# Hybrid decoder layer: the delta rule's queries and later keys projected with tokens in partitions

## The chip, the cores and the metric

The kernel runs on one core of one Trainium2 chip. Its time is device microseconds of one execution; the kernel before took 744.98 us (median of three runs, 744.90 to 745.07). One more execution was profiled, and all durations below come from it. The engines are TensorE (PE in the profile, its weight loads PEld), VectorE (DVE), ScalarE (ACT), GpSimd (POOL) and SyncE (SP); each works through its own instructions in order and they wait for each other by semaphores. SP, ACT and POOL also issue DMAs, each in the order of its own queue.

## The reference, cut to what matters

One decoder layer on 256 tokens of width 2048. The input is normed and multiplied by one wide matrix `w_in`; its columns feed a gated delta rule (8 heads of 128), a block-sparse attention (8 heads of 128) and two sigmoid gates. For the change only the delta rule's queries, keys and values matter:

```
h = rms_norm(x, pre_norm_w)                       # (256, 2048)
gdn_qkv, gdn_z, gdn_b, gdn_a, moba_qkv, moba_z, gate_a, gate_b = split(h @ w_in)
qkv = silu(causal_depthwise_conv(gdn_qkv, conv_w))   # 4 taps along the tokens, per channel
qa, ka, va = split(qkv)                           # 8 heads of 128 each
qa, ka = l2_normalize(qa), l2_normalize(ka)
oa = gated_delta_rule(qa, ka, va, beta, g)        # scores k.k and q.k, a triangular inverse, a recurrence
...
x + rms_norm((sigmoid(gate_a) * u_a + sigmoid(gate_b) * u_b) @ w_out, post_norm_w)
```

The convolution runs along the tokens with one weight per channel and tap, so the kernel wants channels in partitions and tokens along the free axis for it.

## The kernel before, in words

Every product is done in float32r with each operand split into a high and a low part, and three products are summed: high by high, high by low and low by high. The normed input stands in SBUF as `hT`: features in partitions, 16 blocks of 128 features (`KT`), and for each block 512 columns, 256 tokens of the high part and 256 of the low part. The weights come from DRAM in loads of up to 1 MB by SP (`raw`), three buffers in turn. `split` (L260) makes a high part by a copy on ACT (L265) and a low part by a subtraction on DVE (L266), each into one of three buffers, in pieces of 1024 elements a partition. Such a piece is called a split below; a projection of 512 columns of `w_in` has eight, two blocks of 128 features in each. ACT can fill a buffer again when PE has done the split that stood in it three splits ago.

There are two ways to project. `proj_t` (L397) takes 256 columns of `w_in`; the weights are stationary and `hT` streams past, so channels come out in partitions. For each of two heads and each feature block it issues one matmul of 512 columns (high weights by both parts of `hT`) and one of 256 columns (low weights by the high part). `proj_n` (L419) takes 512 columns of `w_in`; here the tokens of `hT` are stationary and the weights stream, so tokens come out in partitions, and for each feature block and each half of the tokens it issues three matmuls of 512 columns. Both accumulate in PSUM.

The delta rule's first four keys are projected at the start together with the norm (`a_k`, not touched). Its eight queries and last four keys go through `proj_t`, two heads at a time. `halves` (L540) adds the two halves of such an accumulator (a copy on ACT, L542, and an addition on DVE, L543); `conv_silu` (L547) multiplies by the norm's factor on DVE (L550), makes four taps (one on ACT, L553, three on DVE, L555) and a SiLU on ACT (L559). The values go through `proj_n` instead: `values` scales the two accumulators into `ga_[:, 2]` (ACT, L865), `by_feature` (L868) transposes them in blocks of 32 by 32 on DVE (L873), writes them to DRAM (`v_t_d`, POOL, L825) and reads them back with channels in partitions (POOL, L829), and `conv_silu` copies each head from there (ACT, L552). When a pair of queries is ready, `score_pair` (L589) splits keys and queries (`kq`, L593 and L594), transposes the queries for their norms, multiplies (`s`, three matmuls of 512 and three of 256 columns a head), scales the products into `gdn` (DVE, L656 to L674), and writes blocks of them to DRAM by four DMAs (`l_d`, POOL, L612), from which `inverse` later builds the triangular inverse on DVE.

The order of the work is the order in which the program is written, and it holds on every engine. The list `ORDER` (L58) gives the projections. Inside a projection `tick()` is called after each piece of it, eight times for 256 columns and sixteen for 512, and each queue of side work (`gq` for scores and inverse, `cq` for values and attention features, and others) is then asked whether its next step is due; a step says by `yield` how long to wait, where 1 is two calls. The waits are constants at the top of the file (`R_WAIT`, `C_WAIT1` to `C_WAIT3`, `SC_WAIT` and others) and are not touched.

Of the kernel before, what the change touches and what calls it, by code (L numbers as in the profile page):

```python
# [8 lines left out]
F32 = mybir.dt.float32  # L9
F32R = mybir.dt.float32r  # L10
BF16 = mybir.dt.bfloat16
AF = mybir.ActivationFunctionType
# [3 lines left out]
P = 128  # L16
# [27 lines left out]
C_WAIT2 = 2.5  # L44
C_WAIT3 = 1
# [10 lines left out]


ORDER = (  # L58
    "q0 mv0 zg0 q1 kq2 kq3 zg1 v0 zm0 v1 zm1 mk0 mk1 mv1 ga0 ga1 ga2 ua0 ua1"
).split()  # L60


# [43 lines left out]
def hybrid_layer(  # L106
# [15 lines left out]
    nc = tc.nc  # L122
    B, S, D = x.shape
    NT = S // P
    KT = D // P
# [29 lines left out]
    def acc_tile(name):  # L155
        return acc.tile([P, 512], F32, tag="acc", name=name)
# [11 lines left out]
    def tick():  # L168
        after[0] -= 0.5
        for q in (gq, vq, mq, aq, bq, *extra):  # L170
            q.tick()
# [3 lines left out]
    def mm(*args, **kwargs):  # L175
        return pin(nc.tensor.matmul(*args, **kwargs))  # L176
# [83 lines left out]
    def split(raw, shape, name):  # L260
        splits[0] += 1
        pool = fourth[0] if fourth and splits[0] % 4 == 0 else wspl
        hi = pool.tile(shape, F32R, tag="hi", name=f"hi_{name}")
        lo = pool.tile(shape, F32R, tag="lo", name=f"lo_{name}")
        nc.scalar.copy(hi, raw)  # L265
        nc.vector.tensor_tensor(lo, raw, hi.bitcast(F32), op=ALU.subtract)  # L266
        return hi, lo
# [126 lines left out]
    na, dtb = nad[:, :H], nad[:, H:]  # L394


    def proj_t(col, name):  # L397

        pts = [acc_tile(f"a_{name}_{m}") for m in range(2)]
        for kb in range(2):  # L400
            raw = wraw.tile([P, 8, 256], F32, tag="raw", name=f"raw_{name}_{kb}")
            nc.sync.dma_start(
                raw, w_in[kb * 1024 : (kb + 1) * 1024, col : col + 256].rearrange("(k p) c -> p k c", p=P)
            )
            for m in range(2):
                hi, lo = split(raw[:, :, m * P : (m + 1) * P], [P, 8, P], f"{name}_{kb}_{m}")
                for k0 in range(0, 8, 2):
                    ks = range(k0, k0 + 2)
                    for kk in ks:
                        k = kb * 8 + kk  # L410
                        mm(pts[m], hi[:, kk, :], hT[:, k, :], start=(k == 0), stop=False)
                    for kk in ks:
                        k = kb * 8 + kk
                        mm(pts[m][:, :S], lo[:, kk, :], hT[:, k, :S], start=False, stop=(k == KT - 1))
                    if k0 % 4 == 2:
                        tick()
        return pts

    def proj_n(w, col, stat, nk, name, width=512, bank=acc_tile):  # L419

        pts = [bank(f"a_{name}_{t}")[:, :width] for t in range(NT)]
        for kb in range(nk // 4):
            raw = wraw.tile([P, 4, width], F32, tag="raw", name=f"raw_{name}_{kb}")
            nc.sync.dma_start(raw, w[kb * 512 : (kb + 1) * 512, col : col + width].rearrange("(k p) c -> p k c", p=P))
            for u in range(2):
                hi, lo = split(raw[:, 2 * u : 2 * u + 2, :], [P, 2, width], f"{name}_{kb}_{u}")
                for kk in range(2):
                    k = kb * 4 + u * 2 + kk
                    for t in range(NT):
                        sh = stat[:, k, t * P : (t + 1) * P]  # L430
                        sl = stat[:, k, S + t * P : S + (t + 1) * P]
                        mm(pts[t], sh, hi[:, kk, :], start=(k == 0), stop=False)
                        mm(pts[t], sh, lo[:, kk, :], start=False, stop=False)
                        mm(pts[t], sl, hi[:, kk, :], start=False, stop=(k == nk - 1))
                    tick()
        return pts
# [103 lines left out]
    def halves(pt, name):  # L540
        y = wf.tile([P, S], F32, tag="f256", name=f"y_{name}")
        nc.scalar.copy(y, pt[:, S:])  # L542
        nc.vector.tensor_tensor(y, pt[:, :S], y, op=ALU.add)  # L543
        return y

    def conv_silu(y, m, late=None, turned=None):
        xp = xps[xpi[0] % 3]  # L547
        xpi[0] += 1
        if turned is None:
            nc.vector.tensor_tensor(xp[:, NTAP - 1 :], y, rrow, op=ALU.mult)  # L550
        else:
            pin(nc.scalar.copy(xp[:, NTAP - 1 :].rearrange("p (t i c) -> p t i c", t=NT, i=4), turned))  # L552
        nc.scalar.activation(y, xp[:, 0:S], AF.Copy, scale=pcol[:, m : m + 1])  # L553
        for j in range(1, NTAP):
            nc.vector.scalar_tensor_tensor(  # L555
                y, xp[:, j : j + S], pcol[:, j * NCV + m : j * NCV + m + 1], y, op0=ALU.mult, op1=ALU.add
            )
        if late is None:
            nc.scalar.activation(y, y, AF.Silu)  # L559
        else:  # L560
            late.append(lambda: pin(nc.scalar.activation(y, y, AF.Silu)))
# [26 lines left out]
    def score_pair(h, kT, qT):  # L588
        kqs = []  # L589
        for m in range(2):  # L590
            kq = big.tile([P, 2, 2 * S], F32R, tag=("tt", "tw")[m], name=f"kq_{h + m}")
            for i, y in enumerate((kT[m], qT[m])):
                nc.scalar.copy(kq[:, i, :S], y)  # L593
                nc.vector.tensor_tensor(kq[:, i, S:], y, kq[:, i, :S].bitcast(F32), op=ALU.subtract)  # L594
            kqs.append(kq)
        yield Q_WAIT[h > 0]
        blocks = ga_[:, D // 512 - 1, h // 2 % 2]
        to = blocks.rearrange("p (j m t c) -> p m t j c", j=4, m=2, t=NT)
        for m in range(2):
            pin(nc.vector.transpose(to[:, m], qT[m].rearrange("p (t r j) -> p t j r", t=NT, j=4)))  # L600
        d = dram.tile([4, P, P], F32, name=f"q_d_{h}")
        nc.gpsimd.dma_start(d.rearrange("i (r j) x -> (i r) (j x)", j=4), blocks)
        q_ds.append(d)
        yield SC_WAIT - Q_WAIT[h > 0]

        for m in range(2):
            yield from scores(h + m, kqs[m])

        for b in range(4):
            t, p_ = b // 2, b % 2  # L610
            c0 = t * 4 * P + p_ * 64
            nc.gpsimd.dma_start(  # L612
                l_d[b, h : h + 2].rearrange("h j i -> j h i"),
                gsl[h // HG][p_ * 64 : p_ * 64 + 64, h % HG : h % HG + 2, c0 : c0 + 64],
            )
# [108 lines left out]

    kTs = [[] for _ in range(H // 2)]

    def keys(p):
        pk = proj_t(CK + 2 * p * P, f"k{2 * p}")
        kTs[p] += [halves(pk[m], f"k{2 * p + m}") for m in range(2)]
        for m in range(2):  # L730
            conv_silu(kTs[p][m], H + 2 * p + m)

    def queries(p):
        h = 2 * p
        pq = proj_t(CQ + h * P, f"q{h}")
        qTs = [halves(pq[m], f"q{h + m}") for m in range(2)]
        for m in range(2):
            conv_silu(qTs[m], h + m)
        gq.add(score_pair(h, kTs[p], qTs))
        if p == H // 2 - 1:  # L740
            gq.add(inverse())
            gq.add(solve())

# [110 lines left out]
            )  # L854

    v_left = [H // 2]

    cq = Queue()
    extra.append(cq)

    def values(g):
        pts = proj_n(w_in, CV + g * 512, hT, KT, f"v{g}")
        x = ga_[:, 2]
        for t in range(NT):
            nc.scalar.activation(x[:, t], pts[t], AF.Copy, scale=rstd[:, t : t + 1])  # L865
        cq.add(v_feat(g, x))

    def by_feature(name, x, blocks):  # L868
        yield C_WAIT1
# [11 lines left out]
    def v_feat(g, x):  # L881
        back = yield from by_feature(f"v{g}", x, ga_[:, 1])
        yield C_WAIT2
        for p in range(2):
            h = 4 * g + 2 * p
            after[0] = SLOW
            vTs = [wf.tile([P, S], F32, tag="f256", name=f"y_v{h + m}") for m in range(2)]
            for m in range(2):
                conv_silu(vTs[m], 2 * H + h + m, turned=back[:, 2 * p + m])
                yield C_WAIT3  # L890
            vq.add(v_tok(h, vTs))
            v_left[0] -= 1
# [529 lines left out]
    nq.add(query_norms())  # L1422
    for blk in ORDER:
        n, c = blk[:2].rstrip("0123456789"), int(blk[-1])
        if n in ("q", "kq"):
            if n == "kq":
                keys(c)
            queries(c)
        elif n in ("zg", "zm"):
            silu_gate(n, c)  # L1430
        elif n == "v":
            values(c)
        elif n == "mv":
            attention_values(c)
        elif n == "mk":
            attention(c)
        elif n == "ua":
            branch_pair(c)
        else:
            sigmoid_gate(n, {"ga": CGA, "gb": CGB}[n], c)  # L1440
# [285 lines left out]
```

## Time and profile before

| | |
|---|---|
| median of three runs | 744.98 us |
| profiled execution | 745.39 us |
| span of its profile | 743.7 us |
| PE busy | 734.3 us (99%), 3594 matmuls |
| DVE busy | 606.8 us (82%) |
| ACT busy | 456.1 us (61%) |
| POOL busy | 90.2 us (12%) |
| TensorE clock | 0.998 of full speed |

The span is what the profile covers, 1.7 us less than the execution's own time. A busy share of PE says that some matmul was under way, not that it ran at its peak: matmuls overlap, so the time that one takes from the next is the distance between their starts, and not the duration that its row gives. The distance is read from a stretch of the chain: its length divided by its matmuls.

### The profile page before, as it was taken

How to read it: one execution, taken by the hardware profiler on the slowest of the kernel's cores; microseconds unless marked ns; L12 is line 12 of the kernel's file. 1: busy time of each engine (PE TensorE's matmuls, PEld its weight loads, DVE VectorE, ACT ScalarE, POOL GpSimd, SP SyncE). 2: the span in 40 equal slices, each digit the busy share in tenths (PEclk: the TensorE clock that was granted, in tenths of full speed). 3: DMA queues.
4: the chain of work that ended last, by engine and by line, in shares of the span. 5: the costliest groups of instructions: out<-in, count | busy, mean ns of one | idle time of the engine just before them, and what ended most of it. 6: DMA issues, size and time to landing. Idle time of an engine off the chain costs nothing.

```text
span 743.7 us, 9927 instructions
## 1 busy us (share of the span) xinstructions
PE 734.3 (99%) x3594; PEld 620.7 (83%) x3594; DVE 606.8 (82%) x957; ACT 456.1 (61%) x692; POOL 90.2 (12%) x124
## 2 busy tenths in 40 slices
PE   9999999999999999999999999999999999999995
PEld 7898998899888888888888888888888888888885
DVE  6887779997896998988547889688797799898864
ACT  6777665556775665547556765657556653875751
POOL 1000301113100101232011050001000101110000
PEclk9999999999999999999999999999999999999999
DMA  8676586548867767988468789798988889998962
GB/s 290 206 233 223 167 239 199 171 153 249 289 215 238 251 200 266 309 295 289 158 216 313 260 301 281 223 343 231 344 224 314 231 299 284 378 346 224 276 244 113
DMA packets 94199, 187.49 MB, mean 252 GB/s; under 512 B 4421, under 2 KB 25606, under 8 KB 93638
## 3 DMA queue, kind: packets, MB, share of 16 engines
q1 hardware_dynamic: 76806, 134.83, 54.5%
q0 software_dynamic: 15584, 47.20, 21.8%
q10 hardware_dynamic: 1760, 4.83, 1.7%
q8 instruction: 28, 0.46, 0.2%
q14 instruction: 21, 0.17, 0.1%
HBM read 173.20 MB, written 13.64 MB: 251 GB/s over the span
## 4 chain that ended last, share of the span: by engine, by line
PE 98%; DMA 1%; DVE 0%; SPq 0%; ACT 0%; DVEq 0%; issue 0%
PE a_ga L176 12%; PE a_gb L176 12%; PE a_y L176 9%; PE a_ub L176 7%; PE a_zg L176 6%; PE a_k L176 6%; PE a_q L176 6%; PE a_mq L176 6%; PE a_mv L176 6%; PE a_mk L176 6%; PE a_v L176 6%; PE a_zm L176 6%; PE a_ua L176 5%; PE s L176 1%; PE po L176 1%; PE so L176 1%
## 5 line engine op out<-in xcount | busy, mean ns | idle before, releaser
L176 PE MATMUL a_ga<-hi_ga,hT 128*128 128x512 f32 x256 | 81.5, 393 | 0.0
L176 PE MATMUL a_gb<-hi_gb,hT 128*128 128x512 f32 x256 | 80.4, 389 | 0.0
L176 PEld LDWEIGHTS a_ga<-hi_ga,hT 128*128 128x128 f32 x256 | 48.1, 188 | 9.9
L176 PEld LDWEIGHTS a_gb<-hi_gb,hT 128*128 128x128 f32 x256 | 48.0, 188 | 9.9
L265 ACT CAST hi_gb<-raw_gb 128x1024 fp32r<-128x1024 f32 x32 | 33.6, 1054 | 29.3 <-PE a_gb L176 15.0
L266 DVE TENSOR_TENSOR lo_ga<-raw_ga,hi_ga 128x1024 fp32r<-128x1024 f32 x32 | 38.9, 1219 | 14.2 <-ACT hi_ga L265 13.9
L176 PE MATMUL a_ga<-lo_ga,hT 128*128 128x512 f32 x128 | 50.0, 390 | 0.0
L176 PE MATMUL a_gb<-lo_gb,hT 128*128 128x512 f32 x128 | 49.9, 390 | 0.0
L176 PE MATMUL a_zg<-hi_zg,hT 128*128 128x348 f32 (+1 forms) x192 | 46.7, 322 | 0.0
L265 ACT CAST hi_ga<-raw_ga 128x1024 fp32r<-128x1024 f32 x32 | 33.4, 1051 | 20.3 <-PE a_ga L176 16.7
L266 DVE TENSOR_TENSOR lo_gb<-raw_gb,hi_gb 128x1024 fp32r<-128x1024 f32 x32 | 38.7, 1215 | 6.9 <-ACT hi_gb L265 6.2
L176 PE MATMUL a_mv<-hi_mv,hT 128*128 128x512 f32 x128 | 41.6, 395 | 0.0
L176 PE MATMUL a_mk<-hi_mk,hT 128*128 128x512 f32 x128 | 40.5, 393 | 0.0
L176 PE MATMUL a_q<-hT,hi_q 128*128 128x512 f32 x128 | 40.2, 396 | 0.0
L176 PE MATMUL a_mq<-hi_mq,hT 128*128 128x512 f32 x128 | 39.8, 390 | 0.0
L176 PE MATMUL a_v<-hi_v,hT 128*128 128x512 f32 x128 | 39.8, 389 | 0.0
L176 PE MATMUL a_zm<-hi_zm,hT 128*128 128x512 f32 x128 | 39.8, 389 | 0.0
L176 PE MATMUL a_k<-hT,hi_k 128*128 128x512 f32 (+1 forms) x129 | 38.5, 398 | 0.7 <-ACT hi_k L297 0.6
L176 PEld LDWEIGHTS a_zg<-hi_zg,hT 128*128 128x128 f32 x192 | 33.5, 188 | 0.1
L266 DVE TENSOR_TENSOR lo_mv<-raw_mv,hi_mv 128x1024 fp32r<-128x1024 f32 x16 | 19.4, 1217 | 17.2 <-ACT hi_mv L265 16.0
L176 PE MATMUL a_zg<-lo_zg,hT 128*128 128x348 f32 (+1 forms) x96 | 30.9, 322 | 0.0
L265 ACT CAST hi_zg<-raw_zg 128x696 fp32r<-128x696 f32 (+1 forms) x24 | 18.5, 771 | 19.7 <-PE a_zg L176 7.4
(479 smaller groups left out, 2022.0 us busy)
## 6 DMA issues: line engine op xcount, KB each, us to landing
raw_ga<-in_w_in_dram SPq DMA_DIRECT2D x16, 1024.0 KB, 6.5
raw_gb<-in_w_in_dram SPq DMA_DIRECT2D x16, 1024.0 KB, 7.3
raw_y<-in_w_out_dram SPq DMA_DIRECT2D x14, 1024.0 KB, 8.7
raw_q<-in_w_in_dram SPq DMA_DIRECT2D x8, 1024.0 KB, 5.6
raw_mv<-in_w_in_dram SPq DMA_DIRECT2D x8, 1024.0 KB, 5.1
raw_v<-in_w_in_dram SPq DMA_DIRECT2D x8, 1024.0 KB, 5.1
raw_zm<-in_w_in_dram SPq DMA_DIRECT2D x8, 1024.0 KB, 5.2
raw_mq<-in_w_in_dram SPq DMA_DIRECT2D x8, 1024.0 KB, 6.2
```

Of the source, the lines that this page charges most:

```text
L176: return pin(nc.tensor.matmul(*args, **kwargs))
L265: nc.scalar.copy(hi, raw)
L266: nc.vector.tensor_tensor(lo, raw, hi.bitcast(F32), op=ALU.subtract)
```

## The change

`proj_t`, `keys`, `queries` and `values` go. One function `project(n, g)` takes their place: it projects four heads (512 columns of `w_in`) by `proj_n`, scales the two accumulators into `ga_` (ACT) and queues a generator. For values that is `v_feat` as before; for queries and keys it is the new `qk_feat`, which lets `by_feature` turn the four heads by DVE and DRAM, waits until the decays are done, and then runs `conv_silu` head by head from the block read back, with a step of waiting after each. A pair of queries then goes to `score_pair` as before. The keys have a queue of their own (`keyq`). `ORDER` puts queries 0 to 3, keys 4 to 7 and queries 4 to 7 first, and the values 0 to 3 between the gate blocks `zg0` and `zg1`.

```
 ORDER = (
-    "q0 mv0 zg0 q1 kq2 kq3 zg1 v0 zm0 v1 zm1 mk0 mk1 mv1 ga0 ga1 ga2 ua0 ua1"
+    "q0 k1 q1 mv0 zg0 v0 zg1 zm0 v1 zm1 mk0 mk1 mv1 ga0 ga1 ga2 ua0 ua1"
 ).split()
...
-    def proj_t(col, name):
-
-        pts = [acc_tile(f"a_{name}_{m}") for m in range(2)]
...
-    def keys(p):
-        pk = proj_t(CK + 2 * p * P, f"k{2 * p}")
-        kTs[p] += [halves(pk[m], f"k{2 * p + m}") for m in range(2)]
-        for m in range(2):
-            conv_silu(kTs[p][m], H + 2 * p + m)
-
-    def queries(p):
-        h = 2 * p
-        pq = proj_t(CQ + h * P, f"q{h}")
-        qTs = [halves(pq[m], f"q{h + m}") for m in range(2)]
-        for m in range(2):
-            conv_silu(qTs[m], h + m)
-        gq.add(score_pair(h, kTs[p], qTs))
-        if p == H // 2 - 1:
+    cq, keyq = Queue(), Queue()
+    extra += cq, keyq
+
+    def project(n, g):
+
+        pts = proj_n(w_in, {"q": CQ, "k": CK, "v": CV}[n] + g * 512, hT, KT, f"{n}{g}")
+        x = ga_[:, 0 if n == "k" else 2]
+        for t in range(NT):
+            nc.scalar.activation(x[:, t], pts[t], AF.Copy, scale=rstd[:, t : t + 1])
+        (keyq if n == "k" else cq).add(v_feat(g, x) if n == "v" else qk_feat(n, g, x))
+
+    def qk_feat(n, g, x):
+        back = yield from by_feature(f"{n}{g}", x, ga_[:, 1])
+        yield C_WAIT2
+        while decaying:
+            yield 0.5
+        for p in range(2 * g, 2 * g + 2):
+            h = 2 * p
+            ys = [wf.tile([P, S], F32, tag="f256", name=f"y_{n}{h + m}") for m in range(2)]
+            for m in range(2):
+                conv_silu(ys[m], (H if n == "k" else 0) + h + m, turned=back[:, h % 4 + m])
+                yield C_WAIT3
+            if n == "k":
+                kTs[p] += ys
+            else:
+                gq.add(score_pair(h, kTs[p], ys))
+        if (n, g) == ("q", 1):
             gq.add(inverse())
             gq.add(solve())
...
-    def values(g):
-        pts = proj_n(w_in, CV + g * 512, hT, KT, f"v{g}")
-        x = ga_[:, 2]
-        for t in range(NT):
-            nc.scalar.activation(x[:, t], pts[t], AF.Copy, scale=rstd[:, t : t + 1])
-        cq.add(v_feat(g, x))
...
-        if n in ("q", "kq"):
-            if n == "kq":
-                keys(c)
-            queries(c)
+        if n in ("q", "k", "v"):
+            project(n, c)
```

Three places of the instructions' order follow. The first is PE, at the start of the first query projection (`a_q_0` and `a_q_1` are its accumulators, `hT_166` the input, `hi_` and `lo_` the parts of the weights). Before:

```order
L176 MATMUL a_q_0_649<-hT_166,hi_q_0_0_653 128x512 x2
L176 MATMUL a_q_0_649<-hT_166,lo_q_0_0_654 128x256 x2
L176 MATMUL a_q_0_649<-hT_166,hi_q_0_0_653 128x512 x2
L176 MATMUL a_q_0_649<-hT_166,lo_q_0_0_654 128x256 x2
L176 MATMUL a_q_0_649<-hT_166,hi_q_0_0_653 128x512 x2
```

And now, at the same place:

```order
L176 MATMUL a_q_0_649<-hi_q_0_0_653,hT_166 128x512
L176 MATMUL a_q_0_649<-lo_q_0_0_654,hT_166 128x512
L176 MATMUL a_q_0_649<-hi_q_0_0_653,hT_166 128x512
L176 MATMUL a_q_1_650<-hi_q_0_0_653,hT_166 128x512
L176 MATMUL a_q_1_650<-lo_q_0_0_654,hT_166 128x512
L176 MATMUL a_q_1_650<-hi_q_0_0_653,hT_166 128x512
```

Two matmuls of 512 and two of 256 columns for two feature blocks of one head have become three of 512 columns for one feature block and half of the tokens, four heads wide.

The second place is POOL's queue around the first scores (`q_d` are queries for their norms, `l_d` blocks of the scores, `gdn` the scaled scores, `tv` an identity for the inverse). Before:

```order
L524 AFFINE_SELECT tv<-one 32x1024 x4
L602 DMA q_d_1102<-ga 128x512
L612 DMA l_d<-gdn_468 64x2x64 x4
L602 DMA q_d_1342<-ga 128x512
L612 DMA l_d<-gdn_468 64x2x64 x4
```

And now (`k_t_d` and `q_t_d` are the blocks of keys and queries that are turned by DRAM; the read-back into `ga` is the line after them or after `l_d`):

```order
L502 AFFINE_SELECT tv<-one 32x1024 x4
L816 DMA k_t_d<-ga 128x1024
L820 DMA ga<-k_t_d 128x4x256
L580 DMA q_d_1136<-ga 128x512
L816 DMA q_t_d<-ga 128x1024
L590 DMA l_d<-gdn_468 64x2x64 x4
L820 DMA ga<-q_t_d 128x4x256
L580 DMA q_d_1365<-ga 128x512
L590 DMA l_d<-gdn_468 64x2x64 x4
```

The write of queries 4 to 7 and their read-back stand on both sides of the first pair's four `l_d` writes; nothing of the kind was in this queue before the values.

The third place is ACT, where the queries behind the first scores are worked up (`hi_` are the casts of L265, `y_q` the queries in work, `kq` their split, `xp` the padded input of the taps). Before, from the last cast of one projection's weights on:

```order
L265 CAST hi_k_1_1_1328<-raw_k_1_1306 128x1024
L559 ACTIVATE y_q_1222<-y_q_1222 128x256
L593 CAST kq_1288<-y_q_1222 128x256
L559 ACTIVATE y_q_1225<-y_q_1225 128x256
L265 CAST hi_q_0_0_1374<-raw_q_0_1372 128x1024
```

And now, from the last cast of the block `mv0` to the first two of `zg0`:

```order
L265 CAST hi_mv_3_1_1399<-raw_mv_3_1373 128x1024
L530 COPY xp_159<-ga 128x256
L530 COPY xp_160<-ga 128x256
L531 ACTIVATE y_q_1391<-xp_159,pcol 128x256
L531 ACTIVATE y_q_1392<-xp_160,pcol 128x256
L265 CAST hi_zg_0_0_1443<-raw_zg_0_1441 128x696
L530 COPY xp_161<-ga 128x256
L531 ACTIVATE y_q_1467<-xp_161,pcol 128x256
L537 ACTIVATE y_q_1391<-y_q_1391 128x256
L537 ACTIVATE y_q_1392<-y_q_1392 128x256
L265 CAST hi_zg_0_1_1475<-raw_zg_0_1441 128x696
```

The copies from the read-back of queries 4 to 7 (`ga`) stand ahead of the first cast of `zg0`, where ACT had only work on data of PE and DVE before.

## Rows read from the trace of the kernel before

**Rows 1.** The page's chain that ended last, its shares by engine.

```profile
PE 98%; DMA 1%; DVE 0%; SPq 0%; ACT 0%; DVEq 0%; issue 0%
```

**Rows 2.** The chain in order of time: start us, length us, matmuls; five of PE's pieces.

```profile
48.58 11.16 PE a_q L176 x64
...
135.12 11.15 PE a_k L176 x64
...
159.51 7.64 PE a_zg L176 x48
...
198.69 21.76 PE a_zm L176 x96
...
263.97 22.02 PE a_mq L176 x96
```

**Rows 3.** The timeline of PE around one head's score products: start us, us, instruction.

```profile
104.28 1.21 PE L176 MATMUL s<-kq 128*128 128x512 f32 x6
105.32 0.63 PE L176 MATMUL a_q<-hT,hi_q 128*128 128x512 f32 x2
```

**Rows 4.** The timeline of ACT at the first values' read-back.

```profile
209.61 1.05 ACT L265 CAST hi_zm<-raw_zm 128x1024 fp32r<-128x1024 f32 x1 [1.66 <-PE a_zm L176]
211.18 0.41 ACT L552 COPY xp<-ga 128x256 f32<-128x256 f32 x1 [0.52 <-DMA ga<-v_t_d]
```

**Rows 5.** Groups of ACT's instructions: busy us, mean ns | idle us before.

```profile
L265 ACT CAST hi_mv<-raw_mv 128x1024 fp32r<-128x1024 f32 x16 | 16.8, 1051 | 13.1 <-PE a_mv L176 13.0
...
L553 ACT ACTIVATE y_q<-xp,pcol 128x256 f32<-128x256 f32 x8 | 4.1, 510 | 1.6 <-DVE xp L550 1.4
...
L593 ACT CAST kq<-y_q 128x256 fp32r<-128x256 f32 x8 | 3.3, 407 | 0.2
...
L552 ACT COPY xp<-ga 128x256 f32<-128x256 f32 x8 | 3.2, 399 | 0.5 <-DMA ga<-v_t_d 0.5
```

**Rows 6.** Groups of DVE's instructions, the same columns.

```profile
L266 DVE TENSOR_TENSOR lo_mv<-raw_mv,hi_mv 128x1024 fp32r<-128x1024 f32 x16 | 19.4, 1217 | 17.2 <-ACT hi_mv L265 16.0 <-PE a_mv L176 1.2
...
L266 DVE TENSOR_TENSOR lo_zg<-raw_zg,hi_zg 128x696 fp32r<-128x696 f32 x16 | 15.2, 956 | 4.5 <-ACT hi_zg L265 4.5
...
L555 DVE SCALAR_TENSOR_TENSOR y_q<-xp,pcol,y_q 128x256 f32<-128x256 f32 x24 | 11.1, 474 | 0.1
L873 DVE STREAM_TRANSPOSE ga<-ga 128x512 f32<-128x512 f32 x10 | 11.0, 1099 | 0.1
...
L666 DVE SCALAR_TENSOR_TENSOR gdn<-s,cj,dec 128x512 f32<-128x512 f32 x8 | 6.0, 749 | 0.2
...
L674 DVE SCALAR_TENSOR_TENSOR gdn<-s,cj,dec 128x256 f32<-128x256 f32 x8 | 3.8, 475 | 0.0
...
L594 DVE TENSOR_TENSOR kq<-y_k,kq 128x256 fp32r<-128x256 f32 x8 | 3.3, 411 | 0.0
...
L656 DVE SCALAR_TENSOR_TENSOR jk<-s,ident 128x128 bf16<-128x128 f32 x8 | 2.3, 283 | 1.0 <-PE s L176 1.0
...
L663 DVE TENSOR_SCALAR cj<-nrm 128x2 f32<-128x2 f32 x8 | 1.3, 162 | 0.1
```

**Rows 7.** The timeline of DVE, three instructions in a row.

```profile
148.63 0.47 DVE L555 SCALAR_TENSOR_TENSOR y_k<-xp,pcol,y_k 128x256 f32<-128x256 f32 x1
149.02 0.41 DVE L550 TENSOR_TENSOR xp<-y_k,rrow 128x256 f32<-128x256 f32 x1
149.36 0.48 DVE L555 SCALAR_TENSOR_TENSOR y_k<-xp,pcol,y_k 128x256 f32<-128x256 f32 x1
```

**Rows 8.** The timeline of POOL: the first `l_d` writes, the first values' read-back.

```profile
118.19 2.40 POOL L612 DMA_DIRECT2D l_d<-gdn  x4 [22.45 <-DVE gdn L666]
...
205.40 0.75 POOL L829 DMA_DIRECT2D ga<-v_t_d  x1 [2.97 <-ACT hi_zm L265]
```

**Rows 9.** All 20 read-backs of L829, from issue to data in place.

```profile
DMA to landing us min/median/max: 3.4/4.9/7.4
```

**Rows 10.** A stretch by engine: us, busy (instructions) of PE, PEld, DVE, ACT, POOL, clock, DMA.

```profile
121.00:145.00 24.00, 24.00 (x140) 20.94 (x139) 23.22 (x53) 14.12 (x24) 2.51 (x5) 1.00 0.68 203
```

More of the change, by code (lines that the diff above doesn't have):

```diff
@@ L394, in hybrid_layer @@
     na, dtb = nad[:, :H], nad[:, H:]
-    def proj_t(col, name):
-        pts = [acc_tile(f"a_{name}_{m}") for m in range(2)]
[L400 to L404, printed above, removed]
-            for m in range(2):
[L406 to L417, printed above, removed]
     def proj_n(w, col, stat, nk, name, width=512, bank=acc_tile):
@@ L725, in hybrid_layer @@
     kTs = [[] for _ in range(H // 2)]
-    def keys(p):
-        pk = proj_t(CK + 2 * p * P, f"k{2 * p}")
-        kTs[p] += [halves(pk[m], f"k{2 * p + m}") for m in range(2)]
-        for m in range(2):
-            conv_silu(kTs[p][m], H + 2 * p + m)
-    def queries(p):
-        h = 2 * p
-        pq = proj_t(CQ + h * P, f"q{h}")
-        qTs = [halves(pq[m], f"q{h + m}") for m in range(2)]
-        for m in range(2):
-            conv_silu(qTs[m], h + m)
-        gq.add(score_pair(h, kTs[p], qTs))
-        if p == H // 2 - 1:
+    cq, keyq = Queue(), Queue()
[22 more added lines that the diff above has]
+        if (n, g) == ("q", 1):
             gq.add(inverse())
@@ L856, in hybrid_layer @@
     v_left = [H // 2]
-    cq = Queue()
-    extra.append(cq)
-    def values(g):
-        pts = proj_n(w_in, CV + g * 512, hT, KT, f"v{g}")
-        x = ga_[:, 2]
-        for t in range(NT):
-            nc.scalar.activation(x[:, t], pts[t], AF.Copy, scale=rstd[:, t : t + 1])
-        cq.add(v_feat(g, x))
     def by_feature(name, x, blocks):
@@ L1424, in hybrid_layer @@
         n, c = blk[:2].rstrip("0123456789"), int(blk[-1])
-        if n in ("q", "kq"):
-            if n == "kq":
-                keys(c)
-            queries(c)
+        if n in ("q", "k", "v"):
+            project(n, c)
         elif n in ("zg", "zm"):
             silu_gate(n, c)
-        elif n == "v":
-            values(c)
         elif n == "mv":
```

## The prediction, made before the changed kernel ran

> **What bounds the kernel now.** I read the chain that ended last first: PE has 98% of it, and no other engine reaches 1% [rows 1]. So the end moves only by what PE computes, or by what makes PE stand. Then the chain in order of time, for what a projection costs. A projection of 256 columns by `proj_t` is 64 matmuls and takes 11.15 to 11.16 us wherever it stands; one of 512 columns by `proj_n` is 96 matmuls and takes 21.76 us, 22.02 us at the dearest; 48 matmuls of a `zg` block take 7.64 us, 0.159 us each [rows 2]. One head's scores hold PE from 104.28 to 105.32, 1.04 us [rows 3]. Third, the timelines of ACT, DVE and POOL for what feeds PE. A cast waits for PE, 1.66 us of 2.72, because its buffer comes free only when PE has finished the split three back [rows 4]; so neither engine can work far ahead of PE, and what holds them longer than about a split reaches PE.
>
> **The change, part by part.** *PE's work.* Six projections by `proj_t` go: 6 x 11.15 = 66.9 us. Three by `proj_n` come: 3 x 21.76 = 65.3 us [rows 2]. The columns streamed are the same number (147,456 in both: 6 x 16 x 2 x 768, and 3 x 16 x 6 x 512), the matmuls are 384 before and 288 now. That is 1.63 us less, 17 ns for each of the 96 matmuls saved. The dear block of 22.02 us would give 66.1 and leave 0.85 us. I take 1.63, since the blocks around it run at 21.76. The score products, the inverse and everything behind `mv1` stay as they are; the scores only stand beside other blocks, at the same 1.04 us a head.
>
> One rule speaks against this term. By the Trainium skill (TensorE: Matmul & The Clock Gate, Back-to-back issue gap) a matmul costs its columns at 2.4 GHz and 2.5 ns; 96 matmuls fewer would then give an estimated 0.24 us. The trace disagrees: the same formula makes 64 such matmuls of `proj_t` 10.4 us, and the rows have 11.15 [rows 2].
>
> *DVE, ACT, POOL and SP beside PE.* DVE loses 24 additions and multiplications of 128x256, whose nearest row is `kq` at 0.41 us (9.9 us), and gains six transposes at 1.10 us (6.6 us) [rows 6]. ACT exchanges twelve copies for twelve copies and gains six scalings. POOL issues six DMAs more, SP as many loads as before. PE covers all of this; without that cover it would cost what the next paragraph finds. That DVE may be full is shown by 24 us in which it is busy for 23.2 and PE for all [rows 10].
>
> *The new wait.* Queries, keys and queries are each turned by DRAM, and ACT's copies from the read-back stand in its queue ahead of casts. For the first queries and the keys this is early enough: more than four splits (11 us) lie between DVE's transposes and the copies, with nothing slow between write and read-back. For queries 4 to 7 it isn't. Their read-back stands in POOL's queue behind the first pair's four `l_d` writes, which wait for DVE's scaling of head 1. Count from S, the moment when PE has done the second split of `mv0` and so frees the buffer for the fifth cast:
> - cast 1.05, one `kq` cast 0.41 [rows 5]; then on DVE `kq` 0.41, `jk` 0.28, `kq` 0.41, three small ones 0.16 each, the low part 1.22, `gdn` 0.75 and 0.48 [rows 6]. That is 5.5 us; where neighbours don't depend on each other each starts about 0.08 us before the last one's end (0.47 long, next one 0.39 later [rows 7]), so I take 5.2.
> - the four `l_d` issues, 2.4 us [rows 8]: S + 7.6.
> - the read-back, 3.4 to 7.4 us, median 4.9 [rows 9]: data at S + 12.5. ACT is through with the eighth cast at S + 3 x 2.72 + 1.05 = S + 9.2 and stands 3.3 us.
> - two copies and a tap on ACT (0.40, 0.40, 0.51 [rows 5], 1.1 with overlap), then DVE until the low part of the third split of `zg0`: 12 taps at 0.474, 3 low parts at 0.956, 2 `jk`, 3 small, 2 `kq`, two `gdn`: 11.7 us, with 24 overlaps 9.7 [rows 6, 7]: S + 23.3.
> - PE comes to that low part after six splits of 2.72, two heads' scores of 1.04, 24 matmuls of 0.159 and one more of 0.16 [rows 2, 3]: S + 22.4.
>
> So PE stands 0.9 us. With a read-back of 3.4 us the low part is there 0.6 us early and PE doesn't stand; with 7.4 it stands 3.4 us. I take the median. What is queued behind the waiting copy is ACT's casts of `zg0`, behind them DVE's low parts, and PE waits for those; short splits of 1.9 us give DVE no time to catch up, so what is lost there stays lost. The values' first read-back before took 5.8 us to ACT's start and made ACT wait 0.52 us at such a place [rows 4, 8], without `l_d` in between.
>
> **The sum.** 0.9 - 1.63 = -0.7 us. The profiled execution took 745.39 us (span 743.7 and 1.7 around it), so 744.7; it is 0.4 us above the median of the runs, 744.98. Against the median I predict 744.3 us.
>
> **The rivals.**
> - *No stall.* The read-back is quick, or DVE's scaling of the first pair comes earlier than I count, or one cast slips ahead; the whole gain stays: 745.0 - 1.6 = 743.35 us. For it: the stall is the small difference of two sums of 22 us, and half of the read-backs are under 4.9 us. Against it: ACT waited already at the values, where nothing stood in between [rows 4]. Chance 0.40.
> - *Forecast*, a stall between 0.15 and 3.1 us: 744.3, its own range 743.5 to 746.4. Chance 0.42.
> - *Slower: POOL's queue.* The read-back waits for `l_d`, and `l_d` for DVE; POOL stood 22.45 us at this write before, which cost nothing as nobody waited behind it [rows 8]. Each microsecond that DVE is later with head 1's scaling than S + 5.2 now is one on PE. It decides from a stall of 3.1 us, which is 2.2 us later than counted; one split of DVE lost there (2.7 us) makes the stall 3.6 and the time 745.0 - 1.6 + 3.6 = 747.0 us. For it: DVE has work for nearly all of PE's time there. Against it: the links from S on are tied to PE's own progress. Chance 0.12.
> - *The change doesn't give what it should.* The new blocks run at 22.02 us, or a matmul has hardly a cost of its own: gain 0.85 or 0.24 us, and with half the stall 744.6 to 745.2 us, no change. Against it: eleven and twenty-two microseconds are the same in all undisturbed blocks [rows 2]. Chance 0.06.
>
> **How the numbers follow.** A measurement of this kernel can tell about 0.2%, 1.5 us, from no change. The whole gain is only 0.14 us above that, so I count 0.8 of the first rival as faster: 0.32. The forecast, the rest of the first rival and the last one are no change: 0.42 + 0.08 + 0.06 = 0.56. Slower: 0.12. The range reaches from a clean gain with 0.25 us more from smoother starts of blocks, 743.1, to the forecast with a stall of 2.8 us, 746.2; outside lie the slower rival and little else.
>
> **What would show it.** Each of the chain's three pieces for `a_q` and `a_k` (without the first block) should sum to 21.8 us, and PE's matmuls should be 96 fewer. ACT should show a wait at the copies into `xp` for the read-back of `q_t_d`, of about 3 us, with POOL's read-back right behind four `l_d` issues. PE should stand in the third split of `zg0`, near 144 to 146 us, waiting for its low part on DVE; if PE is idle nowhere the first rival holds. It is wrong if PE waits elsewhere: for the keys' read-back inside the second query block, or later, when the inverse and the values' taps share DVE.

## The result, and the profile after

The changed kernel takes 752.76 us (median of 4 runs, 752.57 to 754.19), the kernel before beside it 745.03 us: 1.0107 times as long, with an interval from 1.0089 to 1.0124. The prediction was 744.3 us, no change, with a range up to 746.2 us; the kernel got slower by 7.7 us. The profiled execution took 754.19 us, its span is 752.5 us, 8.8 us more than before. Two single executions lie far outside all others, 1240 us of kernel 8 and 1914 us of experiment 13, and are left out of the ratios.

The chain that ended last no longer belongs to TensorE alone. The page's line of shares answers to [rows 1]:

```profile
PE 54%; DVE 11%; DMA 3%; issue 2%; ACT 2%; DVEq 0%; POOL 0%; POOLq 0%; ACTq 0%
```

The view of who waited for whom, for TensorE, in the changed kernel (total us, times, longest us); before it has none of these:

```profile
PE a_zm L176 <- DVE lo_zm L266: 2.6, 3, 1.2
PE a_ga L176 <- DVE lo_ga L266: 1.3, 2, 0.9
...
PE a_zg L176 <- DVE lo_zg L266: 1.1, 2, 0.8
PE a_mq L176 <- DVE lo_mq L266: 0.9, 2, 0.6
PE a_ua L176 <- DVE lo_ua0p L266: 0.5, 1, 0.5
```

Since the ends of matmuls are modelled, I measured the standing from their starts. In a block that is not held up the starts lie 0.227 us apart at 512 columns (21.76 us for 96, [rows 2]), 0.16 us at 348, 0.12 us at 256 and 0.08 us at 128. Wherever two starts lie over 0.1 us further apart than that, the excess is counted as standing; over the whole timeline of TensorE it is 7.1 us before and 17.0 us after. The difference of 10.0 us, less the 1.63 us of matmul work that the prediction took off, is 8.3 of the 8.8 us that the span grew. Of the 10.0 us, some 9.6 lie in five places. Another 0.8 us stand near 655 us; the profiled execution was the longest of the four, and in the traces of kernels 3, 4, 5 and 8 nothing stands there. The five places alone, less 1.63, give 7.9 us, close to the 7.7 of the medians. The table gives the standing in us, taken the same way from every trace (the kernels are those of the experiments below; "ga2, ua0" counts the blocks' own matmuls and not the attention products between them):

| place | before | after | v0 after zg1 | sums sooner | both | l_d moved, turn sooner | that, with the change's order |
|---|---|---|---|---|---|---|---|
| zg0 | 0 | 2.6 | 2.8 | 2.6 | 2.2 | 0 | 0 |
| zm0 | 0 | 2.6 | 0 | 2.5 | 0 | 0 | 2.4 |
| end of zm1, start of mq0 | 0.2 | 1.5 | 0.1 | 1.3 | 0.1 | 0.1 | 1.1 |
| mq1 | 0.3 | 1.1 | 0.9 | 1.2 | 0.9 | 0.9 | 1.2 |
| ga2, ua0 | 0.3 | 2.6 | 2.8 | 0.3 | 0.3 | 0.3 | 0.3 |
| all starts | 7.1 | 17.0 | 12.3 | 14.1 | 9.5 | 7.6 | 11.1 |
| median, us | 745.0 | 752.8 | 748.8 | 750.9 | 746.4 | 744.1 | 748.6 |

**zg0, the predicted place.** Timeline of GpSimd in the changed kernel: write, four l_d writes, read-back of queries 4 to 7:

```profile
123.50 0.55 POOL L816 DMA_DIRECT2D q_t_d<-ga  x1 [16.79 <-DVE jk L634]
126.84 2.43 POOL L590 DMA_DIRECT2D l_d<-gdn  x4 [2.79 <-DVE gdn L644]
129.26 0.78 POOL L820 DMA_DIRECT2D ga<-q_t_d  x1
```

ScalarE's and VectorE's timelines behind it, and TensorE's where it stands longest (one fence each):

```profile
135.05 0.71 ACT L530 COPY xp<-ga 128x256 f32<-128x256 f32 x2 [4.03 <-DMA ga<-q_t_d]
```

```profile
136.21 2.47 DVE L533 SCALAR_TENSOR_TENSOR y_q<-xp,pcol,y_q 128x256 f32<-128x256 f32 x6 [3.93 <-ACT y_q L531]
```

```profile
146.09 0.43 PE L176 MATMUL a_zg<-lo_zg,hT 128*128 128x348 f32 x1 [0.84 <-DVE lo_zg L266]
```

The read-back goes out as the l_d writes end, lands 5.8 us later, VectorE is without work for 3.93 us and then busy without a gap until 152.9 us. TensorE pays for it in the third split of zg0, at 146 us, as predicted.

**zm0, where the unit order changed.** The first values (v0) stood behind zg1; now they stand ahead of it. Windows of the changed kernel (us, busy and instructions of PE, PEld, DVE, ACT, POOL, then clock, DMA share, GB/s):

```profile
190.00:192.00 2.00, 2.00 (x14) 2.00 (x13) 0.89 (x1) 0.85 (x2) 0.90 (x2) 1.00 1.05 389
...
198.00:200.00 2.00, 2.00 (x13) 1.87 (x12) 1.73 (x4) 0.55 (x1) 1.42 (x2) 1.00 1.04 383
...
204.00:206.00 2.00, 2.00 (x10) 1.67 (x9) 1.04 (x3) 2.00 (x6) 0.00 (x0) 1.00 1.03 401
```

All eight windows from 190 to 206 us have a DMA share of 0.94 or more (the share counts a packet in the window where it starts, so it can pass 1). What landed late is in ScalarE's timeline there, and in the tile view of raw_zm:

```profile
200.66 1.05 ACT L265 CAST hi_zm<-raw_zm 128x1024 fp32r<-128x1024 f32 x1 [2.12 <-DMA raw_zm<-in_w_in_dram]
203.80 0.71 ACT L530 COPY xp<-ga 128x256 f32<-128x256 f32 x2 [2.09 <-DMA ga<-v_t_d]
```

```profile
DMA to landing us min/median/max: 5.3/8.8/9.4
```

Before, the same four loads took 4.9/5.3/7.8 us. They also go out closer together now. SyncE's timeline in the changed kernel and in kernel 3, which has the old order:

```profile
187.79 12.41 SPq L402 DMA_DIRECT2D raw_zm<-in_w_in_dram  x4
```

```profile
183.05 16.39 SPq L402 DMA_DIRECT2D raw_zm<-in_w_in_dram  x4
```

VectorE's and TensorE's timelines show how the late values reach TensorE: as in zg0, the taps stand ahead of a split's low part.

```profile
204.96 2.87 DVE L533 SCALAR_TENSOR_TENSOR y_v<-xp,pcol,y_v 128x256 f32<-128x256 f32 x7 [1.99 <-ACT y_v L531]
207.74 1.22 DVE L266 TENSOR_TENSOR lo_zm<-raw_zm,hi_zm 128x1024 fp32r<-128x1024 f32 x1
```

```profile
209.01 0.50 PE L176 MATMUL a_zm<-lo_zm,hT 128*128 128x512 f32 x1 [1.21 <-DVE lo_zm L266]
```

**ga2 and ua0, 260 us later.** The sums of the branch's weights end in an accumulating DMA. GpSimd's timeline, before and after:

```profile
444.13 1.32 POOL L947 DMA_DIRECT2D tq_z<-in_w_branch_a_dram  x1 [5.23 <-DVE tq_g L944]
```

```profile
455.94 1.33 POOL L928 DMA_DIRECT2D tq_z<-in_w_branch_a_dram  x1 [10.43 <-DVE tq_g L925]
```

This DMA is 11.8 us later than before. The load of raw_ga that followed it by 9.4 us before (453.54 us) is only 5.6 us later, and now goes out 3.2 us behind it. SyncE's and ScalarE's timelines of the changed kernel:

```profile
459.14 9.89 SPq L968 DMA_DIRECT2D raw_ga<-in_w_in_dram  x2
```

```profile
469.13 1.05 ACT L265 CAST hi_ga<-raw_ga 128x1024 fp32r<-128x1024 f32 x1 [5.20 <-DMA raw_ga<-in_w_in_dram]
```

The lateness can be followed back on GpSimd: the fetch for the sums 394.77 and 405.80 us (11.0 later), the inverse's first write-out 328.50 and 336.31 (7.8), the last l_d write 174.41 and 183.96 (9.6).

### The profile page after: what moved, and what is told of

The parts are those of the page before. It is cut to its first block, busy times and chain, and to the rows that moved or that the text cites. A ratio compares the mean times of both kernels' runs of the same rounds, so it can differ in the third digit from the quotient of the medians.

```text
span 752.5 us, 9724 instructions
## 1 busy us (share of the span) xinstructions
PE 736.5 (98%) x3498; PEld 615.8 (82%) x3498; DVE 602.8 (80%) x939; ACT 458.3 (61%) x698; POOL 93.8 (12%) x130
## 3 DMA queue, kind: packets, MB, share of 16 engines
q10 hardware_dynamic: 1760, 4.83, 1.7%
## 4 chain that ended last, share of the span: by engine, by line
PE 54%; DVE 11%; DMA 3%; issue 2%; ACT 2%; DVEq 0%; POOL 0%; POOLq 0%; ACTq 0%
PE a_gb L176 12%; PE a_y L176 9%; PE a_ga L176 8%; PE a_ub L176 7%; PE a_mq L176 5%; PE a_ua L176 5%; PE a_mv L176 3%; PE a_mk L176 3%; DVE tw L760 1%; DVE lo_ga L266 1%; DVE tv L767 1%; DVE lo_mk L266 1%; DMA ga<-v_t_d 1%; DVE lo_v L266 1%; DMA raw_ga<-in_w_in_dram 1%
## 5 line engine op out<-in xcount | busy, mean ns | idle before, releaser
L265 ACT CAST hi_ga<-raw_ga 128x1024 fp32r<-128x1024 f32 x32 | 33.4, 1049 | 28.8 <-PE a_ga L176 17.3
L265 ACT CAST hi_gb<-raw_gb 128x1024 fp32r<-128x1024 f32 x32 | 33.6, 1054 | 27.7 <-PE a_gb L176 13.3
L176 PE MATMUL a_q<-hi_q,hT 128*128 128x512 f32 x128 | 40.1, 391 | 0.0
L176 PEld LDWEIGHTS a_ga<-lo_ga,hT 128*128 128x128 f32 x128 | 24.1, 188 | 7.1 <-DVE lo_ga L266 2.3
L265 ACT CAST hi_zg<-raw_zg 128x696 fp32r<-128x696 f32 (+1 forms) x24 | 18.4, 770 | 18.8 <-PE a_zg L176 13.2
L176 PEld LDWEIGHTS a_gb<-lo_gb,hT 128*128 128x128 f32 x128 | 24.0, 188 | 5.4 <-DVE lo_gb L266 0.4
```

## The experiments

All start from the changed kernel or from one another; times are medians, and ratios are to the kernel before, run beside them. A unit of waiting, two calls of `tick()`, is one split of TensorE work, 2.72 us at 512 columns and 1.9 us in the zg blocks (expectation 1 says two splits; its 2.72 us is one).

**1. Later taps for queries 4 to 7.**

```diff
-        yield C_WAIT2
+        yield 4 if (n, g) == ("q", 1) else C_WAIT2
```

> Against the changed kernel (752.8 us) one number differs: the taps of queries 4 to 7 are issued 4 units after their read-back instead of 2.5 (a unit is two splits, 2.72 us of TensorE), 4.1 us later; in the trace ScalarE stood 4.03 us at the copy into xp. Theory A, a late landing: only the order in which ScalarE and VectorE meet the read-back is wrong, so the 2.7 us that TensorE stands in zg0 go: 750.1 us, all other stalls as they are. Theory B, full engines: the transposes, copies, taps and splits of that stretch are too much for VectorE and ScalarE together, and the stall moves into the next splits: 752.8 us, with the same 2.7 us of standing a few us later.

752.17 us, 1.0092 [1.0078, 1.0106], not to be told from the change by time. In the trace 2.6 us in zg0 became 1.7, at 148 to 151 us. That is between the theories. VectorE's idle time from 129 to 139 us fell only from 4.7 to 3.8 us; that the work left undone then makes the later stall is argued, not shown.

**2. Later taps for the values.**

```diff
-        yield C_WAIT2
+        yield 4          # in v_feat
```

> Against the changed kernel one number differs: the taps of both groups of values are issued 4 units after their read-back instead of 2.5. In the trace ScalarE stood 2.1 us at the first group's copy and up to 3.4 us at the second's, and TensorE lost 2.6 us in zm0 and 1.5 us at the end of zm1 and the start of mq0. Theory A (late landings): both go, 752.8 - 4.1 = 748.7 us, or up to 1 us more where the inverse, which waits for the last values, ends later. Theory B (the inverse and the values' taps fill VectorE): the stalls stay, 752 to 753 us.

753.79 us, 1.0121 [1.0100, 1.0143]: both expectations missed. The stalls around mq0 and in mq1 went, but 6.0 us stood in zm0. The first copies kept their place in time and now stood ahead of the third cast, which the change has ahead of them. ScalarE's timeline:

```profile
203.81 0.71 ACT L530 COPY xp<-ga 128x256 f32<-128x256 f32 x2 [3.13 <-DMA ga<-v_t_d]
...
205.24 1.03 ACT L265 CAST hi_zm<-raw_zm 128x1024 fp32r<-128x1024 f32 x1
```

A wait by count moves everything that the scheduler places by it, not the one copy. Of the 6.0 us 1.8 are the clock (last section).

**3. The first values where they were.**

```diff
-    "q0 k1 q1 mv0 zg0 v0 zg1 zm0 v1 zm1 mk0 mk1 mv1 ga0 ...
+    "q0 k1 q1 mv0 zg0 zg1 v0 zm0 v1 zm1 mk0 mk1 mv1 ga0 ...
```

> Against the changed kernel only the unit order differs: the first values are projected after zg1, where the kernel before had them, so that their turn is past the inverse's first DMAs (l_d, lc) and the read-backs of the queries' norms (q_d), which in the changed kernel lie within 10 us of the first values' read-back. If the order made the 2.6 us in zm0, those go: 750.2 us, the stalls of zg0 and of the gates and the branch (ga2, ua0) as they are. If the projection of queries and keys in natural form made them, by taking the time in which the inverse ran, they stay: 752.8 us.

748.82 us, 1.0039 [1.0027, 1.0052]: 4 us, more than the 2.6 expected, since the 1.5 us around mq0 went too. zg0 and ga2 stand as before this edit. raw_zm's tile view is as before the change again:

```profile
DMA to landing us min/median/max: 4.9/5.4/7.6
```

**4. The weight sums sooner.**

```diff
-T_WAIT = (15, 2, 4, 4)
+T_WAIT = (13, 2, 4, 4)
```

> Against the changed kernel one number differs: the first sums of the branch's weights are issued 13 units after their fetch instead of 15, 5.4 us sooner. In the trace the accumulating DMA that follows them (tq_z) was issued at 455.94 us, 3.2 us before the load of raw_ga that took 9.9 us to land and at which ScalarE stood 5.2 us; before, it was issued 9.4 us ahead of that load, which took 5.0 us. Theory A (the two transfers share the DMA engines because the inverse ends 6 us later in the program): the load lands sooner, the 2.5 us that TensorE lost at 464 to 476 us go, 750.3 us. Theory B (the sums on VectorE and the casts on ScalarE fill those engines there): no better than 752.5 us.

750.88 us, 1.0076 [1.0064, 1.0088], and 0.3 us stand at ga2 and ua0, as before the change. GpSimd's and ScalarE's timelines: the accumulating DMA goes out 7 us sooner, and the cast that waited 5.20 us waits 0.87.

```profile
448.92 1.33 POOL L928 DMA_DIRECT2D tq_z<-in_w_branch_a_dram  x1 [3.36 <-DVE tq_g L925]
```

```profile
464.01 1.05 ACT L265 CAST hi_ga<-raw_ga 128x1024 fp32r<-128x1024 f32 x1 [0.87 <-DMA raw_ga<-in_w_in_dram]
```

**5. Both.** Edits 3 and 4 together.

> The changed kernel with both edits that gained: the first values after zg1, and the weight sums issued at 13 units instead of 15. If the places are separate, their gains add: 748.8 us with the order alone, less some 2.4 us that still stood at ga2 and ua0 there, 746.4 us; what is left is the 2.7 us in zg0 and some 0.7 us at the start of mq1. If the gain of the sums needed the late inverse of the other order, 748.8 us.

746.43 us, 1.0012 [1.0003, 1.0021]. The places add up; what is left is zg0 and mq1.

**6 to 9. The read-back of queries 4 to 7.** Four kernels, all with edits 3 and 4: l_d's first writes from GpSimd's queue or from ScalarE's, the turn in its place or half a unit sooner, the taps at the same time.

```diff
-        yield C_WAIT2
+        yield 3 if (n, g) == ("q", 1) else C_WAIT2      # 3.5 with the sooner turn
-            nc.gpsimd.dma_start(
+            (nc.gpsimd if h else nc.scalar).dma_start(  # l_d moved: 7 and 8
-        yield C_WAIT1
+        yield 0.5 if name == "q1" else C_WAIT1          # turn sooner: 8 and 9
```

6, l_d on GpSimd, the turn in its place:

> As the kernel with both edits (first values after zg1, sums at 13 units), and the taps of queries 4 to 7 issued at 3 units instead of 2.5, which puts only the first copy and its tap behind the last split of mv0 and lets a split of zg0 in between two heads. It is the partner of the next kernel. If TensorE's 2.7 us in zg0 come from VectorE's 4 us without work before the landing at 135 us, the stall stays within 0.7 us: 745.8 to 746.5 us.

7, l_d on ScalarE, the turn in its place:

> As the kernel before it in this list (taps at 3 units), but the first head pair's four writes of l_d are issued from ScalarE's queue and not from GpSimd's, so that GpSimd can issue the queries' read-back as soon as their write has landed; all other queues keep their order. In the trace the read-back was issued at 129.26 us, at the end of the four writes, and landed at 135.05. Theory A (the predicted place, GpSimd's queue): it is issued some 2 us sooner, at about 127.2 us, lands at about 133 us, and 1.5 to 2.5 us of the 2.7 us in zg0 go, 744 to 745 us. Theory B (the stretch is too full for VectorE whenever the data come): within 0.5 us of the kernel before it.

8, l_d on ScalarE, the turn sooner:

> As the kernel before it in this list, and VectorE turns queries 4 to 7 half a unit (1.36 us) sooner after their projection, so that write and read-back come 1.4 us sooner too, while the taps keep their place. Theory A (a late landing): what was left in zg0 shrinks by another 0.5 to 1 us, 743.5 to 744.5 us, under the 745.0 us of the kernel before the change. Theory B (a full VectorE): no gain, since the transposes only change places with splits.

9, l_d on GpSimd, the turn sooner:

> As the kernel that reached 744.1 us (first values after zg1, sums at 13 units, queries 4 to 7 turned half a unit sooner with taps at 3.5 units), but with the first head pair's l_d writes in GpSimd's queue again, where the changed kernel has them. With the sooner turn the read-back was issued at 123.10 us, 4 us before those writes can start (their data are there at 127 us). If the queue mattered only because the four writes stood between write and read-back, the sooner turn alone does it only if the queue's order changes with it; here the order stays write, l_d, read-back, so the read-back waits for the scores again until 129 us: 745.5 to 746.5 us. If the sooner turn was all that counted: 744.1 us.

| | l_d on GpSimd | l_d on ScalarE |
|---|---|---|
| turn as in the change | 747.86 us, 1.0033 [1.0021, 1.0045] | 746.09 us, 1.0015 [1.0006, 1.0024] |
| turn half a unit sooner | 747.78 us, 1.0035 [1.0023, 1.0047] | 744.14 us, 0.9990 [0.9979, 1.0001] |

GpSimd's timeline at the read-back, in the kernels 6, 7, 9 and 8:

```profile
129.41 0.78 POOL L820 DMA_DIRECT2D ga<-q_t_d  x1
```

```profile
127.52 0.76 POOL L820 DMA_DIRECT2D ga<-q_t_d  x1 [3.85 <-DMA q_t_d<-ga]
```

```profile
117.72 0.55 POOL L816 DMA_DIRECT2D q_t_d<-ga  x1 [10.73 <-DVE ga L854]
126.86 2.42 POOL L590 DMA_DIRECT2D l_d<-gdn  x4 [8.59 <-DVE gdn L644]
129.27 0.78 POOL L820 DMA_DIRECT2D ga<-q_t_d  x1
```

```profile
123.10 0.76 POOL L820 DMA_DIRECT2D ga<-q_t_d  x1 [4.81 <-ACT kq L571]
```

ScalarE's timeline at the first copy, in kernel 7 and in kernel 8:

```profile
134.15 0.41 ACT L530 COPY xp<-ga 128x256 f32<-128x256 f32 x1 [3.19 <-DMA ga<-q_t_d]
```

```profile
131.28 0.40 ACT L530 COPY xp<-ga 128x256 f32<-128x256 f32 x1
```

In kernel 9 the turned queries are written at 117.72 us, 6 us sooner than in the change (1.4 were expected), and are still read back at 129.27, because the queue's order is write, l_d, read-back and l_d's data come at 126.86. In kernel 8 the same write is read back at 123.10, the copy doesn't wait, and nothing stands in zg0. With the sooner turn, moving the l_d writes is worth 3.6 us. With the turn in its place it is worth 1.8 us by time, since the write itself lands at 127.5. By the starts kernel 6 stands 3.3 us in zg0, 7 2.9, 9 2.8 and 8 none: neither edit alone takes the stall away, both together do. The 0.5 us between 6 and 7 don't explain their 1.8 us; kernel 6's profiled execution was its longest.

Only kernel 8 came out as expected. Kernel 6, which differs from kernel 5 by half a unit of the taps alone, took 1.4 us more than kernel 5; kernels 6 and 9 took 1.3 to 1.4 us more than the range expected, and kernel 7 lost 0.5 us of its stall where 1.5 to 2.5 were expected. Moved to ScalarE, the writes also wait there for VectorE ahead of the last two casts of mv0, and go by another DMA queue (q10 has 2,336 packets in kernel 8, 1,760 in the change). Putting the read-back ahead of the l_d writes in GpSimd's queue would have changed the order alone; that was not run.

**10. Closer scores.** Kernel 8 with `SC_WAIT = 3.5` for 4.

> As the kernel that reached 744.1 us, with each head pair's scores half a unit sooner after the pair's start, which brings the inverse some 4 us forward in the program. What that kernel lost against its TensorE work beyond what the kernel before lost was 0.5 us at the start of mq1, where VectorE had larger steps of a later inverse between two splits. If the late inverse is the cause: 743.6 us. If the closer scores crowd VectorE in zg0 and zg1 again: 745 us or more.

744.59 us, 0.9991 [0.9982, 1.0000]: neither. The inverse's write-out came 3 us sooner and the 0.9 us at mq1 went, but 0.7 us stood at mq0 and 0.4 us in mk1 in its place.

**11. The sums back.** Kernel 8 with `T_WAIT = (15, 2, 4, 4)`.

> As the kernel that reached 744.1 us, but with the weight sums at 15 units as in the changed kernel. It tells whether the 2.5 us at ga2 and ua0 are a place of their own: the inverse is as late there as with 13 units, so the accumulating DMA should again be issued some 3 us before the load of raw_ga: 744.1 + 2.4 = 746.5 us. If that stall only followed from the earlier ones, 744.1 us.

745.71 us, 1.0008 [0.9998, 1.0017], 1.6 us more than kernel 8; 2.1 us stand at ga2 and ua0 again, 2.4 were expected. ScalarE's timeline has the wait back:

```profile
461.50 1.05 ACT L265 CAST hi_ga<-raw_ga 128x1024 fp32r<-128x1024 f32 x1 [4.72 <-DMA raw_ga<-in_w_in_dram]
```

**12. The change's order back.** Kernel 8 with the order line of the change.

> The kernel that reached 744.1 us with one thing put back, the change's unit order (first values before zg1). If the order costs by itself what the first order run showed (2.6 us in zm0, 1.5 us around the start of mq0), 744.1 + 4.1 = 748.2 us, with zg0 and ga2 without stalls. If those 4 us only came from the lateness of queries 4 to 7, which is mended here, under 745.5 us.

748.62 us, 1.0046 [1.0032, 1.0060], as expected: 2.4 us in zm0, 1.1 around mq0. The order costs its 4 us by itself.

**13. Which transfer in zm0.** The queries' norms read back 12 units after the last scores, for 5, in the changed kernel. It was run twice; the trace is the second run's.

```diff
-        yield QN_WAIT
+        yield 12         # once, ahead of the norms' loop
```

> Against the changed kernel one number differs: the read-backs of the queries' norms (q_d, 0.5 MB) wait 12 units instead of 5 after the last scores, which puts them in GpSimd's queue behind the first values' whole turn. In the changed kernel they were issued at 197.92 us, right behind the first values' read-back (197.14), in a stretch from 190 to 206 us in which the DMA engines had no idle share left, and ScalarE stood 2.1 us for raw_zm and 2.1 us for the read-back. Theory A (the unit order packs too many transfers into that stretch): 0.5 MB at the 390 GB/s of the stretch are 1.3 us, both landings come up to 1.3 us sooner, and of TensorE's 2.6 us in zm0 about half goes, 751 to 752 us. Theory B (VectorE and ScalarE alone, the landings don't matter): 752.8 us and the same stall.

> The same kernel as the one whose norms' read-backs (q_d, 0.5 MB) wait 12 units instead of 5, for its trace. If the packed transfers make the stall in zm0: raw_zm and the first values' read-back land up to 1.3 us sooner than in the changed kernel (there ScalarE stood 2.12 us and 2.09 us at them), and the 2.6 us in zm0 shrink to 1 to 2 us; the total by its first three comparable runs (751.6 to 754.1 us) is 751.5 to 752.5 us. If VectorE and ScalarE alone make it: 2.6 us as before.

751.90 us (three executions), 1.0101 [1.0085, 1.0116], and 753.51 us, 1.0110 [1.0096, 1.0124]: neither can be told from the change. Its norms are read back at 216.14 us, after the stretch, and the DMA share from 190 to 204 us is still 0.98 or more. ScalarE's timeline and raw_zm's tile view:

```profile
203.93 0.71 ACT L530 COPY xp<-ga 128x256 f32<-128x256 f32 x2 [2.17 <-DMA ga<-v_t_d]
```

```profile
DMA to landing us min/median/max: 5.1/7.1/8.6
```

The loads come 1.7 us sooner in the median, the values do not, and 2.3 us stand in zm0 for 2.6. So the norms' read-backs are not what makes the stall.

## Why the prediction was wrong

**TensorE's work: right.** The trace after has 3,498 matmuls, 96 fewer. In kernel 8 the span is 742.3 us against 743.7: 1.4 us less, or 1.9 without the 0.5 us that its starts stand more (7.6 us in all, 7.1 before), where 1.63 were worked out. Its chain in order of time has the new blocks undisturbed, at the length of [rows 2]:

```profile
70.92 21.76 PE a_k L176 x96
92.69 21.76 PE a_q L176 x96
```

The Trainium skill (TensorE: Matmul & The Clock Gate, Back-to-back issue gap) gives the rule that the prediction cites for a matmul by itself, and for a stream of weight loads and matmuls about 131 ns at 512 columns. The rule, by which the term would have been an estimated 0.24 us, disagrees with both rows and span; the 227 ns that the rows give at 512 columns agree with neither figure.

**The new wait: right in kind, too small.** "The four `l_d` issues, 2.4 us" took 2.43, and the read-back stands right behind them, as the order of GpSimd's queue let one see. The size came out too small, and the changed kernel's timelines show where, counted from S, which is 120.70 us, the start of the fifth cast (ScalarE, VectorE, TensorE):

```profile
120.70 1.06 ACT L265 CAST hi_mv<-raw_mv 128x1024 fp32r<-128x1024 f32 x1 [1.24 <-PE a_mv L176]
129.97 1.05 ACT L265 CAST hi_mv<-raw_mv 128x1024 fp32r<-128x1024 f32 x1 [1.71 <-PE a_mv L176]
```

```profile
122.13 1.08 DVE L854 STREAM_TRANSPOSE ga<-ga 128x512 f32<-128x512 f32 x1
126.46 0.48 DVE L652 SCALAR_TENSOR_TENSOR gdn<-s,cj,dec 128x256 f32<-128x256 f32 x1
```

```profile
120.50 1.20 PE L176 MATMUL s<-kq 128*128 128x512 f32 x6
```

- Head 1's scaling ended at S + 6.2 us and not S + 5.2: a transpose of queries 4 to 7 themselves, 1.08 us, stands in VectorE's queue ahead of it, and the count left it out.
- The landing took 5.8 us, where the median of [rows 9], 4.9, was taken.
- The eighth cast ended at S + 10.3 and not S + 9.2, since a head's scores stand on TensorE right behind the second split. So ScalarE stood 4.0 us and not 3.3.
- The low part of zg0's third split was ready at S + 25.3 and not S + 23.3. TensorE did three heads' scores on the way to it and not two, and would have been there at S + 23.2 and not S + 22.4.

These give 2.1 to 2.2 us up to the third split, and TensorE stood 2.6 us in all, not 0.9: 0.5 us in the first split, 1.7 in the third, which was counted, and 0.4 behind it. 2.6 us lie within the bounds of 0 to 3.4 us that the step gave; by this alone the time would have been 745.0 - 1.6 + 2.6 = 746.0 us, inside the range. Kernel 5, with the order and the sums mended, took 746.43 us, just past it. Kernels 6 to 9 show that the stall comes from two things together: the l_d writes between write and read-back, and the late write itself.

**"PE covers all of this": this step failed,** with its companion that "the score products, the inverse and everything behind `mv1` stay as they are". It priced what VectorE, ScalarE and GpSimd do by its sum, and put the unit order, which is a line of the change, at nothing.
- The order put the first values' turn into the last splits of zg1 and the first of zm0. Their write, their read-back and the larger loads of zm0 met there with the inverse's first reads. This cost 3.9 us (kernel 3) to 4.5 us (kernel 12), for which the prediction had nothing. That the DMA engines had no share left there, and that loads and values landed late, is shown; which transfer is one too many is not. It is not the norms' read-backs (13). That the four loads of raw_zm go out within 12.4 us, for 16.4 in kernel 3, was not tested by itself.
- Queries 4 to 7 come late, and with them the last scores, the inverse and the weight sums. The sums' wait is counted from their fetch, the loads on SP's queue are not, so the two met. TensorE stood 2.6 us there, some 320 us behind the changed code, and the time it cost is 1.9 us by kernel 4 and 1.6 us by kernel 11.
- Under a microsecond at mq1 comes with the inverse's larger steps between two splits. Experiment 10 moved it and gained nothing, so this is only argued.

The text named, as what would make it wrong, that TensorE waits "later, when the inverse and the values' taps share DVE". That is the place in zm0, and a part of the cause: VectorE had about 1 us in every 2 free from 202 to 206 us, until the data had landed, and then ran seven taps of the values, 2.87 us, ahead of the low part for which TensorE waited. But it gave the place no price, and no chance among the rivals.

**The rivals.** "POOL's queue" had the mechanism in GpSimd's queue and 747.0 us, for one more split lost there; the time went past it by the order and the sums. "No stall" is what kernel 8 reaches: 744.14 us, expected 743.35 for a change without any stall, and by its interval not to be told from the kernel before.

## What to carry to other kernels

Where several engines share one DMA queue, read what stands between a write and its read-back: a write that waits for its own data holds the read-back, however soon the first write landed (3.6 us here, with the sooner turn). When an order of units changes, list the transfers of the moved unit's whole turn and look in the DMA share of the stretch where they will fall, and follow each delayed chain to the next transfer that is placed by a count of work, since that one meets a load that didn't move. A gain of 1.6 us of TensorE's work is given only if every such place is mended: here it took edits at five places in the code (the order, the sums' wait, the l_d writes' queue, the turn, the taps) to get back 8.6 us.

## What the hardware showed that I had not expected

With a DMA share near 1.0 for 16 us a load of 1 MB took 8.8 us in the median, and 5.4 us where the share had gaps; the accumulating DMA beside it made a load take 10.0 us instead of 5.0.

In experiment 2 TensorE stood 1.63 and 2.19 us within 5 us, and then ran at a lower granted clock, 0.57 in the mean from 209 to 213 us, near the lower of its two levels. Its timeline and window there (in the window's row the instruction counts stand in brackets, the clock behind POOL's):

```profile
209.01 0.74 PE L176 MATMUL a_zm<-lo_zm,hT 128*128 128x512 f32 x1 [2.19 <-DVE lo_zm L266]
```

```profile
209.00:213.00 4.00, 3.99 (x11) 3.14 (x12) 3.93 (x8) 3.95 (x15) 0.75 (x1) 0.57 0.43 118
213.00:217.00 4.00, 4.00 (x19) 3.32 (x18) 3.80 (x8) 3.00 (x11) 1.30 (x2) 1.00 0.78 271
```

Eleven matmuls instead of nineteen, by the 0.227 us of each 1.8 us lost after the waits had ended. In the changed kernel itself, whose longest wait in these blocks was 1.2 us, no window of the stretches read shows a clock below 1.00.
